# One normalisation for the four mLSTM heads, its factors spread through DRAM, and copied sums of a third projection

## The chip, the cores and the metric

The kernel runs on one core of a Trainium2 chip. Five engines work beside each other, each with its own queue of instructions in a fixed order: TensorE (PE in the profile, with PEld for its weight loads), VectorE (DVE), ScalarE (ACT), GpSimd (POOL) and SyncE (SP). PE multiplies matrices and writes its sums to PSUM, which has eight banks of 128 partitions x 512 float32 numbers. DVE and ACT read PSUM and SBUF, the on-chip memory. SP and POOL here mostly issue transfers between DRAM and SBUF. The metric is device time in microseconds (us); less is better.

## The reference

One layer of a decoder with two token mixers side by side, for 512 tokens of 1024 features in float32:

```python
u = rms_norm(h, norm_mix_g)
z = u @ w_in                      # q, k, v of both mixers and their gates
ya = moba_attention(...)          # 8 heads x 64
hb = mlstm_chunkwise(...)         # 4 heads x 128: num / max(|den|, exp(-m))
hb = hb * rsqrt(mean(hb * hb, axis=-1) + 1e-6)
yb = sigmoid(ob) * (hb * mlstm_norm_g)
merged = sigmoid(ga) * (ya @ w_proj_a) + sigmoid(gb) * (yb @ w_proj_b)
h = h + merged @ w_out
h = h + (silu(g) * up) @ w_down   # g, up = rms_norm(h) @ w_gate_up
return rms_norm(h, norm_final_g)
```

The change is at the second mixer's norm (hb) and at the two products with w_proj. Because the norm divides by the root of the mean square of num / den, the division by den needn't be done by itself: the factor of a token and head is one over the root of (sum of num squared + eps x 128 x max(den squared, floor)), up to powers of two. The floor, exp(-2 m), is a row of 512 numbers for each head.

## The kernel before, in words

All products are taken in three parts, with each float32 operand split into a high and a low half (`split_hl`: ACT copies the high half, DVE subtracts it). The activations lie with features on the partitions and the 512 tokens along the row.

The program is a list of 66 weight units (`UNITS`): q, k, v, ob, qkb, then eight of ga, fourteen half units gs, eight projections p and eight of wo, and behind these the feed-forward network. `fill(1)` issues the next unit on PE: 24 matmuls of 512 columns in most, 12 in a gs unit. The weights' splits run some units ahead on ACT and DVE. Between the units stands the work of the mixers: generators in a list (`add`, `advance`, `drain`), called at written places. From the first stage on, a scheduler orders each engine's instructions by their place in the program and by its own estimate of when their inputs are there; `add_manual_dep(..., behind)` forces an order on one engine, `issue_after` likewise. What it settled is fixed: on the chip every engine goes through its queue in that order.

PSUM is handed out in three pools: `mmb` (3 banks) for units, `sb` (3 banks) for small products, `accb` (2 banks). The gs units hold two of the `sb` banks (Z) from the first S1 product to S4, so one is left in that time.

The mLSTM (lines 1751 to 1853). `ml_load(h)` (1756) fetches a head's rows from the DRAM tensor scr, broadcast to 128 partitions: 1280 numbers of decay weights in three parts, and the floor's 512. `ml_a` and `ml_c` make the weights and the products num (in `accb`) and den (in `sb`; a product with ones, so all 128 partitions hold the same row). Then for each head:

- `ml_d1` (1823): ACT squares num and den and copies num to nsb; DVE takes the maximum of den squared and the floor; the square of num is split.
- `ml_d2` (1832): two matmuls with ones sum the square over the partitions (L1834, L1835); DVE adds eps x 128 x den squared (L1837); ACT takes Ln and Exp for a first inverse root; three DVE instructions of a Newton step (L351 to L353) and one product with nsb (L1843) follow.
- `ml_e` (1846): the sigmoid of ob, the product with the norm's weight and ob (L1852), and the split into yb.

Heads 0 and 1 go through `ml_d2` inside the loop over the mixers' steps, heads 2 and 3 after it (lines 1915 to 1918), with two gs units issued ahead of them; then one unit, `ml_e` of head 0, one unit, `ml_e` of head 1, and so on.

The gs units make gate B by a scheme of seven products (W11, S1, S2, W12, S3, S4, W22, two units each). The results are read from PSUM by ACT or DVE, turned by DVE, written to DRAM by POOL (gd, L663) and read back (gb, L669), in two groups of four.

The projections (`run_p`, 699) take two banks of `mmb` each, pa = ya @ w and pb = yb @ w. `merge` (686) multiplies them by the gates (L689 reads pa, L692 reads pb), adds and splits; `gate` (676) makes the next one's sigmoids. For the first two, ACT first copies pa and pb to SBUF, and both merges come behind the second one's copies; later ones are merged out of PSUM.

Of the kernel before, what the change touches and what calls it, by code (L numbers as in the profile page):

```python
# [8 lines left out]
F32 = mybir.dt.float32  # L9
F32R = mybir.dt.float32r  # L10
BF16 = mybir.dt.bfloat16
AF = mybir.ActivationFunctionType
ALU = mybir.AluOpType
AX = mybir.AxisListType.X

P = 128
S = 512
# [3 lines left out]
BH = 4  # L21
DFF = 2816
FT = DFF // P
EPS = 1e-6
# [15 lines left out]

RS = [slice(0, 512), slice(512, 896), slice(896, 1280), slice(1280, 1792)]
RW = 1792

KR = [(0, slice(0, 512)), (1, slice(0, 384)), (2, slice(0, 256)), (2, slice(256, 384))]

# [8 lines left out]
PORD = (4, 5, 6, 7, 0, 1, 2, 3)  # L54
# [44 lines left out]
def hybrid_layer_kernel(ctx: ExitStack, tc, xT, wall, wgb, wgc, wgu, wds, wdl, g3v, vecs, wgates, consts, rope, out):  # L99
    nc = tc.nc  # L100
    V, A, T = nc.vector, nc.scalar, nc.tensor
# [7 lines left out]
    dram = ctx.enter_context(tc.tile_pool(name="dr", bufs=1, space=bass.MemoryType.DRAM))  # L109
# [7 lines left out]
    def slot(dt=F32, name="a"):  # L117
        return act.tile([P, S], dt, name=nm(name), tag="A")

    def slot4(dt=F32, name="f"):  # L120
        return act.tile([P, 4, S], dt, name=nm(name), tag="A4", bufs=NA4)
# [25 lines left out]
    raw_ins = lambda i: getattr(i, "ins", i)  # L147
# [12 lines left out]
    def act_(out_, in_, func, **kw):  # L160
        if func not in SETS:
            return A.activation(out_, in_, func, **kw)  # L162
        table(SETS[func])
        if ph["manual"]:
            return A.activation(out_, in_, func, **kw)
        with tc.issue_after(ph["load"]):
            i = A.activation(out_, in_, func, **kw)
        ph["ins"].append(raw_ins(i))
        return i

    def split_hl(src, name="h", dst=None):

        h, l = dst or (slot(F32R, name + "h"), slot(F32R, name + "l"))
        last["a"] = act_(h, src, AF.Copy)
        last["v"] = V.tensor_tensor(l, src, f(h), op=ALU.subtract)  # L175
        return h, l
# [171 lines left out]
    def newton(r, v, new, scale=1.0):  # L348

        t = new()  # L350
        V.tensor_tensor(t, r, r, op=ALU.mult)  # L351
        V.scalar_tensor_tensor(t, v, -0.5 * scale, t, op0=ALU.mult, op1=ALU.mult)
        V.scalar_tensor_tensor(t, t, 1.5, r, op0=ALU.add, op1=ALU.mult)  # L353
        return t
# [30 lines left out]
    def drain(g=None):  # L385
        while bulk and (g is None or g in bulk):
            advance()

    def add(g):
        bulk.append(g)  # L390
        return g


    def fill(n=1, mid=None):

        for _ in range(n):
            u = pos[0]
            if u >= len(UNITS):
                if mid:
                    mid()  # L400
                return
            kind, i = UNITS[u]
            while wstate["split"] <= min(u + LOOK + (kind == "gs"), NGEN - 1):
                split_unit()
            pos[0] += 1
            v = u if u < G0 else max(u + G0, 2 * u - 2 * len(GW)) // 2
            make_sums(5 * (min(v, G0) - 19 + max(v - G0 - 10, 0)) // 4)
            g = run[kind](i, *whl.pop(u))
            next(g, None)
            if mid:  # L410
                mid()
            for _ in g:
                pass
# [141 lines left out]
    def silu_batch(idx):  # L555
        for i in idx:
            a = conv[i]
            act_(a, a, AF.Silu)
        table(SETS[AF.Exp])
        for i in idx:  # L560
            if i < 4:
                st["qk", i] = slot4(F32R, "qk")
            t, o = st["qk", i % 4], 2 * (i // 4)
            qkm[i] = split_hl(conv.pop(i), dst=(t[:, o, :], t[:, o + 1, :]))
            yield
# [21 lines left out]
    def load_x():  # L587
        for n, c in (("A", slice(0, 4)), ("B", slice(4, 8))):
            gs[n] = slot4(name="c" + n)
            nc.gpsimd.dma_start(gs[n], xT[c].rearrange("k p s -> p k s"))  # L590
        yield

    def combine():

        for k in range(4):
            x, v = gs["A"][:, k], gs["B"][:, k]
            ng = ng1[:, k : k + 1]
            with tc.issue_after(raw_ins(last["a"])), tc.issue_after(raw_ins(last["v"])):
                act_(v, v, AF.Copy, scale=col(G1 + k + 4))
                V.tensor_tensor(x[:, A_], x[:, A_], x[:, B_], op=ALU.subtract)  # L600
            V.scalar_tensor_tensor(x[:, B_], x[:, B_], ng, v[:, B_], op0=ALU.mult, op1=ALU.add)
            V.scalar_tensor_tensor(v[:, B_], x[:, A_], ng, v[:, B_], op0=ALU.mult, op1=ALU.subtract)
            V.scalar_tensor_tensor(v[:, A_], v[:, B_], -1.0, v[:, A_], op0=ALU.mult, op1=ALU.subtract)
            yield
# [94 lines left out]
    def run_p(m, wh, wl):  # L699
        if m in PORD[4:]:  # L700
            load_xr()
        pa, pb = mmb(), mmb()
        mm3(pa, wh, wl, range(4), [t[0] for t in ya], [t[1] for t in ya], True, True)
        if m == PORD[0]:
            tc.add_manual_dep(raw_ins(st["first"]), raw_ins(st["gs"]).name, behind, reason="order")
        mm3(pb, wh, wl, range(4, 8), [t[0] for t in yb], [t[1] for t in yb], True, True)
        yield
        if m in PORD[:2]:
            q = slot(name="pa"), slot(name="pb")
            for t, z in zip((pa, pb), q):  # L710
                last["g"] = act_(z, t, AF.Copy)
            early.append((m, *q))
            if m == PORD[1]:
                gate(PORD[0])
                for x in early:
                    merge(*x)
        else:
            merge(m, pa, pb)
# [1035 lines left out]
    sc_b = 128.0 ** -0.5  # L1754

    def ml_load(h):
        t = slot4(name="R").rearrange("p b t -> p (b t)")[:, 0:RW]
        nc.gpsimd.dma_start(t, scr[h : h + 1, :].partition_broadcast(P))
        rbc[h] = [t[:, c] for c in RS]

    def ml_w(h):

        ml_load(h)
        yield
        r = rbc[h]
        c = lambda j: cS[:, 4 * j + h : 4 * j + h + 1]
        for j in range(4):
            w = r[KR[j][0]][:, KR[j][1]]
            w = w[:, 0:P]
            V.scalar_tensor_tensor(w, mmask, c(j), w, op0=ALU.subtract, op1=ALU.min)  # L1770
        yield
        for j in range(4):
            w = r[KR[j][0]][:, KR[j][1]]
            act_(w, w, AF.Exp, bias=c(j))
        wready.add(h)
# [29 lines left out]
    def ml_c(h, b, ats):  # L1805
# [12 lines left out]
        if b == 1:  # L1818
            acc[("d", h)] = sb()
            for i in range(2):  # L1820
                T.matmul(acc[("d", h)], onesr, ats[1][i], start=i == 0, stop=i == 1)

    def ml_d1(h):
        num, den = acc.pop(("n", h)), acc.pop(("d", h))
        sqn, d2, nsb = slot(name="sqn"), slot(name="d2"), slot(name="nsb")
        act_(sqn, num, AF.Square)
        act_(d2, den, AF.Square)
        act_(nsb, num, AF.Copy)
        V.tensor_tensor(d2, d2, rbc[h][3], op=ALU.max)
        return split_hl(sqn, "sq"), d2, nsb  # L1830

    def ml_d2(h, sqn, d2, nsb):
        ps = sb()
        T.matmul(ps, onesr, sqn[0], start=True, stop=False)  # L1834
        T.matmul(ps, onesr, sqn[1], start=False, stop=True)  # L1835

        V.scalar_tensor_tensor(d2, d2, EPS * 128.0, ps, op0=ALU.mult, op1=ALU.add)  # L1837

        r = slot(name="ri")
        act_(r, d2, AF.Ln, scale=2.0**-39)  # L1840
        act_(r, r, AF.Exp, scale=-0.5)
        t = newton(r, d2, lambda: slot(name="nt"), 2.0**-39)
        V.scalar_tensor_tensor(t, t, 2.0**-16, nsb, op0=ALU.mult, op1=ALU.mult)  # L1843
        return t

    def ml_e(h, t):

        ob = gz.pop(("ob", h))
        if h >= 2:
            V.tensor_tensor(ob, ob, rb, op=ALU.mult)  # L1850
        act_(ob, ob, AF.Sigmoid)
        V.scalar_tensor_tensor(t, t, col(MG + h), ob, op0=ALU.mult, op1=ALU.mult)  # L1852
        yb[h] = split_hl(t, dst=pair4("yb", h))

# [5 lines left out]

    fill(1)
    qa, qb = [], []
    norms, norms_out = [], {}
    n = 0

    def norm_d2(h, a1):
        norms_out[h] = ml_d2(h, *a1)
        yield

    LA, LC = 3, 1  # L1870
    todo = {
        1: [rope_group("q", 1)], 3: [rope_group("k", 1)], 13: [ml_w(0)], 14: [silu_batch([0, 4, 1, 5])], 16: [ml_w(2)],
        17: [ml_w(1)], 18: [silu_batch([2, 6, 3, 7])], 19: [ml_w(3)], 20: [load_x()], 25: [combine()],
    }
    while n < len(steps) or qa or qb:
        if qa and (len(qa) >= LA or n >= len(steps)):
# [36 lines left out]
    for i in range(4):  # L1913
        ya[i] = split_hl(ya[i], dst=pair4("ya", i))
    fill(2)
    while norms:
        add(norm_d2(*norms.pop(0)[:2]))
    drain()
    for h in range(4):
        if UNITS[pos[0]][0] != "p":  # L1920
            fill(1)
        ml_e(h, norms_out[h])
    while pos[0] < len(UNITS) and UNITS[pos[0]][0] != "p":
        fill(1)
    ffn()
# [100 lines left out]
```

## Time and profile before

| | |
|---|---|
| median of 3 runs | 724.52 us (724.13 to 725.64) |
| the profiled execution | 721.74 us |
| its span, first to last instruction | 720.0 us |
| busy PE / DVE / ACT / POOL | 702.3 / 617.6 / 460.5 / 84.4 us |
| DMA | 170.52 MB, 237 GB/s on average |
| PE busy from 250 to 300 us, and granted clock | 45.49 of 50 us, 0.93 |
| PE busy from 300 to 350 us, and granted clock | 47.79 of 50 us, 1.00 |

Times in the profile count from the span's start. A row in order of time gives start, duration, engine, line, operation, output and inputs, and in brackets how long the engine was idle before it and what released it. Names leave out buffer numbers: `s`, `mm` and `acc` are banks of the three PSUM pools, `d` is a head's den squared, `nt` the Newton tile, `R` the rows that a head loads. PE's rows overlap, since matmuls are pipelined: their distance in time is from start to start.

### The profile page before, as it was taken

To read this page: it belongs to the slowest core of one execution; us is meant where nothing else is said; L and a number is where in the kernel's file an instruction comes from. 1 tells how busy PE (TensorE), PEld (TensorE's weight loads), DVE (VectorE), ACT (ScalarE), POOL (GpSimd) and SP (SyncE) were. 2 spreads that over 40 slices of the span, in tenths; PEclk is the share of its full clock that TensorE was granted. 3 is DMA by queue.
4 is the path that set the end of the run, shared out by engine and by line. 5 is a ranking of instruction groups with operands and counts; after the bars stand their busy time and mean duration, and the time that the engine had idled before them with its cause. 6 is when DMAs were issued, how large, how long until landed. Compare 5 with 4: busy or idle time off the path is not lost.

```text
span 720.0 us, 9618 instructions
## 1 busy us (share of the span) xinstructions
PE 702.3 (98%) x3248; PEld 582.7 (81%) x3248; DVE 617.6 (86%) x1024; ACT 460.5 (64%) x788; POOL 84.4 (12%) x119
## 2 busy tenths in 40 slices
PE   9999999999999989989999999999999999999995
PEld 6888888887888767878888888878888888888884
DVE  6788977898978699958599898898899799797996
ACT  6634888769766598546354756666765666675664
POOL 0013010000011000122020110013003004003000
PEclk9999999999999998999999999999999999999999
DMA  8769595479989783598999548999979649969703
GB/s 322 289 194 237 185 246 170 165 222 319 233 239 341 209 229 117 201 371 262 320 329 271 168 154 226 364 314 266 357 212 275 230 142 216 315 157 272 221 1 117
DMA packets 50849, 170.52 MB, mean 237 GB/s; under 512 B 6348, under 2 KB 6740, under 8 KB 45296
## 3 DMA queue, kind: packets, MB, share of 16 engines
q1 hardware_dynamic: 38320, 124.67, 49.2%
q0 software_dynamic: 12192, 44.69, 28.0%
q8 instruction: 25, 0.41, 0.2%
q10 hardware_dynamic: 288, 0.56, 0.2%
q14 instruction: 24, 0.20, 0.1%
HBM read 145.73 MB, written 64.00 MB: 291 GB/s over the span
## 4 chain that ended last, share of the span: by engine, by line
PE 71%; DVE 17%; ACT 5%; issue 4%; DMA 2%; DVEq 0%; ACTq 0%
PE mm L223 6%; PE mm L227 6%; PE mm L226 5%; PE mm L1009 5%; PE mm L1008 5%; PE mm L1007 5%; PE s L1009 3%; PE s L1008 3%; PE s L1007 3%; PE mm L1252 2%; PE mm L1255 2%; PE mm L1253 2%; DVE wl L175 2%; PE mm L330 2%; DMA cB<-in_xT_dram 2%
## 5 line engine op out<-in xcount | busy, mean ns | idle before, releaser
L162 ACT ACTIVATE w<-raw 128x1024 fp32r<-128x1024 f32 (+2 forms) x107 | 108.1, 1023 | 46.1 <-PE mm L1008 18.9
L982 DVE TENSOR_TENSOR w<-raw,w 128x1024 fp32r<-128x1024 f32 x70 | 84.3, 1219 | 21.7 <-ACT w L162 19.9
L175 DVE TENSOR_TENSOR wl<-raw,wh 128x1024 fp32r<-128x1024 f32 x62 | 75.0, 1216 | 13.3 <-ACT wh L162 12.5
L162 ACT ACTIVATE wh<-raw 128x1024 fp32r<-128x1024 f32 x62 | 65.2, 1055 | 31.8 <-PE mm L226 20.5
L1007 PE MATMUL mm<-w,bq 128*128 128x512 f32 x160 | 62.2, 389 | 0.0
L1009 PE MATMUL mm<-w,bq 128*128 128x512 f32 x160 | 62.2, 389 | 0.0
L1008 PE MATMUL mm<-w,bq 128*128 128x512 f32 x160 | 62.2, 389 | 0.0
L223 PE MATMUL mm<-u,wh 128*128 128x512 f32 x96 | 37.9, 395 | 0.4 <-ACT ga L162 0.4
L227 PE MATMUL mm<-u,wh 128*128 128x512 f32 x96 | 37.5, 391 | 0.0
L226 PE MATMUL mm<-u,wl 128*128 128x512 f32 x96 | 37.5, 390 | 0.0
L227 PE MATMUL mm<-ul,wh 128*128 128x512 f32 x96 | 37.4, 389 | 0.0
L223 PE MATMUL mm<-uh,wh 128*128 128x512 f32 x96 | 37.4, 389 | 0.0
L226 PE MATMUL mm<-uh,wl 128*128 128x512 f32 x96 | 37.3, 389 | 0.0
L1008 PEld LDWEIGHTS mm<-w,bq 128*128 128x128 f32 x160 | 30.0, 188 | 6.3
L1007 PEld LDWEIGHTS mm<-w,bq 128*128 128x128 f32 x160 | 30.1, 188 | 6.2
L1009 PEld LDWEIGHTS mm<-w,bq 128*128 128x128 f32 x160 | 30.0, 188 | 6.2
L1252 PE MATMUL mm<-w,ac 128*128 128x512 f32 x80 | 31.3, 391 | 0.5 <-ACT w L162 0.5
L1163 DVE TENSOR_TENSOR w<-raw,w 128x1024 fp32r<-128x1024 f32 x25 | 30.3, 1216 | 1.3 <-ACT w L162 1.2
L1253 PE MATMUL mm<-w,ac 128*128 128x512 f32 x80 | 31.2, 390 | 0.0
L1007 PE MATMUL s<-w,bq 128*128 128x512 f32 x80 | 31.1, 389 | 0.0
L1008 PE MATMUL s<-w,bq 128*128 128x512 f32 x80 | 31.1, 389 | 0.0
L1009 PE MATMUL s<-w,bq 128*128 128x512 f32 x80 | 31.1, 389 | 0.0
(492 smaller groups left out, 2030.3 us busy)
## 6 DMA issues: line engine op xcount, KB each, us to landing
raw<-in_wall_dram SPq DMA_DIRECT2D x48, 512.0 KB, 5.8
raw<-ws SPq DMA_DIRECT2D x38, 512.0 KB, 6.4
raw<-in_wgc_dram SPq DMA_DIRECT2D x30, 512.0 KB, 7.1
ws<-in_wgc_dram SPq DMA_DIRECT2D x10, 1024.0 KB, 9.8
ws<-in_wgc_dram POOLq DMA_DIRECT2D x10, 1024.0 KB, 11.2
raw<-in_wds_dram SPq DMA_DIRECT2D x15, 512.0 KB, 8.3
ws<-in_wds_dram SPq DMA_DIRECT2D x10, 512.0 KB, 8.3
ws<-in_wds_dram POOLq DMA_DIRECT2D x10, 512.0 KB, 8.5
```

The lines of the kernel that those rows point to most:

```text
L162: return A.activation(out_, in_, func, **kw)
L175: last["v"] = V.tensor_tensor(l, src, f(h), op=ALU.subtract)
L223: st["mm"] = T.matmul(ps, wh[:, c], rh[j], start=start and j == 0, stop=False)
L226: T.matmul(ps, wl[:, c], rh[j], start=False, stop=False)
L227: T.matmul(ps, wh[:, c], rl[j], start=False, stop=stop and j == n - 1)
L982: V.tensor_tensor(l, t, f(h), op=ALU.subtract)
L1007: st["mm"] = T.matmul(ps[t], bh, wh[:, d], start=first and k == 0, stop=False, skip_group_check=not first)
L1008: T.matmul(ps[t], bh, wl[:, d], start=False, stop=False, skip_group_check=not first)
L1009: T.matmul(ps[t], bl, wh[:, d], start=False, stop=k == 3, skip_group_check=not first)
L1163: V.tensor_tensor(w[k][1], g[k], f(w[k][0]), op=ALU.subtract)
L1252: T.matmul(ps, bh, wh[:, d], start=first and k == 0, stop=False, skip_group_check=not first)
L1253: T.matmul(ps, bl, wh[:, d], start=False, stop=False, skip_group_check=not first)
```

## The change

1. `ml_load` leaves the floor out (1280 numbers of a row instead of 1792). A new generator `floors`, behind `load_x` at step 20, loads the four floors into one tile, 32 partitions for each head, by four transfers on POOL's queue.
2. `ml_d1` squares den for its head's 32 partitions of a tile for all four (den4). `ml_d2` keeps only the two matmuls and an ACT copy of the sum's 32 partitions into a tile for all four (ssq4). For heads 2 and 3 the matmuls are ordered behind the last gs matmul issued so far.
3. `ml_norm` makes the maximum, the sum, Ln, Exp and the Newton step once, on the tiles for four heads. It writes one partition of each head to DRAM (8 KB) and reads that back to all 128 partitions for all four heads (1 MB), both on POOL's queue.
4. `ml_e` multiplies nsb by its head's factor (that was the end of `ml_d2`), and goes on as before.
5. The order: two gs units, head 2's sum, one unit, head 3's sum, one unit, `ml_norm`, one unit; then a unit and an `ml_e` for each head. So `ml_e` of head 0 stands behind the seventh gs unit instead of the fourth.
6. The first three projections' sums are copied by ACT instead of the first two, and the first gates and merges come behind the third one's copies.

```diff
-        if m in PORD[:2]:
+        if m in PORD[:3]:
...
-            if m == PORD[1]:
+            if m == PORD[2]:
...
-        t = slot4(name="R").rearrange("p b t -> p (b t)")[:, 0:RW]
-        nc.gpsimd.dma_start(t, scr[h : h + 1, :].partition_broadcast(P))
+        t = slot4(name="R").rearrange("p b t -> p (b t)")[:, 0:RL]
+        nc.gpsimd.dma_start(t, scr[h : h + 1, 0:RL].partition_broadcast(P))
...
+    def floors():
+        row4["m"] = slot(name="fl4")
+        for h in range(BH):
+            nc.gpsimd.dma_start(row4["m"][32 * h : 32 * h + 32, :], scr[h : h + 1, RS[3]].partition_broadcast(32))
+        yield
...
     def ml_d1(h):
...
-        act_(d2, den, AF.Square)
+        act_(row4["d"][r], den[r], AF.Square)
         act_(nsb, num, AF.Copy)
-        V.tensor_tensor(d2, d2, rbc[h][3], op=ALU.max)
...
     def ml_d2(h, sqn):
...
+        if h >= 2:
+            tc.add_manual_dep(raw_ins(i), raw_ins(st["gs"]).name, behind, reason="order")
         T.matmul(ps, onesr, sqn[1], start=False, stop=True)
-        V.scalar_tensor_tensor(d2, d2, EPS * 128.0, ps, op0=ALU.mult, op1=ALU.add)
-        r = slot(name="ri")
-        act_(r, d2, AF.Ln, scale=2.0**-39)
-        act_(r, r, AF.Exp, scale=-0.5)
-        t = newton(r, d2, lambda: slot(name="nt"), 2.0**-39)
-        V.scalar_tensor_tensor(t, t, 2.0**-16, nsb, op0=ALU.mult, op1=ALU.mult)
+        act_(row4["s"][r], ps[r], AF.Copy)
+    def ml_norm():
+        den4, ssq4 = row4["d"], row4["s"]
+        V.tensor_tensor(den4, den4, row4["m"], op=ALU.max)
+        V.scalar_tensor_tensor(den4, den4, EPS * 128.0, ssq4, op0=ALU.mult, op1=ALU.add)
+        act_(ssq4, den4, AF.Ln, scale=2.0**-39)
+        act_(ssq4, ssq4, AF.Exp, scale=-0.5)
+        t = newton(ssq4, den4, lambda: row4["m"], 2.0**-39)
+        d = dram.tile([BH, S], F32, name="nd4")
+        nc.gpsimd.dma_start(d, t.rearrange("(h r) t -> h r t", r=32)[:, 0, :])
+        row4["b"] = slot4(name="nb4")
+        nc.gpsimd.dma_start(row4["b"], d.rearrange("h t -> (h t)").partition_broadcast(P).rearrange("p (h t) -> p h t", h=BH))
     def ml_e(h):
...
+        t = row4["n", h]
+        V.scalar_tensor_tensor(t, row4["b"][:, h], 2.0**-16, t, op0=ALU.mult, op1=ALU.mult)
         V.scalar_tensor_tensor(t, t, col(MG + h), ob, op0=ALU.mult, op1=ALU.mult)
...
-        1: [rope_group("q", 1)], ..., 20: [load_x()], 25: [combine()],
+        1: [rope_group("q", 1)], ..., 20: [load_x(), floors()], 25: [combine()],
...
     fill(2)
+    drain()
     while norms:
+        fill(1)
         add(norm_d2(*norms.pop(0)[:2]))
-    drain()
+        drain()
+    fill(1)
+    ml_norm()
+    fill(1)
     for h in range(4):
         if UNITS[pos[0]][0] != "p":
             fill(1)
-        ml_e(h, norms_out[h])
+        ml_e(h)
```

More of the change, by code (lines that the diff above doesn't have):

```diff
@@ L42 @@
 RW = 1792
+RL = 1280
 KR = [(0, slice(0, 512)), (1, slice(0, 384)), (2, slice(0, 256)), (2, slice(256, 384))]
@@ L1756, in ml_load @@
     def ml_load(h):
-        t = slot4(name="R").rearrange("p b t -> p (b t)")[:, 0:RW]
-        nc.gpsimd.dma_start(t, scr[h : h + 1, :].partition_broadcast(P))
-        rbc[h] = [t[:, c] for c in RS]
+        t = slot4(name="R").rearrange("p b t -> p (b t)")[:, 0:RL]
+        nc.gpsimd.dma_start(t, scr[h : h + 1, 0:RL].partition_broadcast(P))
+        rbc[h] = [t[:, c] for c in RS[:3]]
     def ml_w(h):
@@ L1821, in ml_c @@
                 T.matmul(acc[("d", h)], onesr, ats[1][i], start=i == 0, stop=i == 1)
+    row4 = {}
+    def floors():
[3 more added lines that the diff above has]
+        yield
     def ml_d1(h):
         num, den = acc.pop(("n", h)), acc.pop(("d", h))
-        sqn, d2, nsb = slot(name="sqn"), slot(name="d2"), slot(name="nsb")
+        sqn, nsb = slot(name="sqn"), slot(name="nsb")
+        r = slice(32 * h, 32 * h + 32)
@@ L1826, in ml_d1, with ml_d2 @@
         act_(sqn, num, AF.Square)
-        act_(d2, den, AF.Square)
+        if h == 0:
+            row4["d"] = slot(name="den4")
+        act_(row4["d"][r], den[r], AF.Square)
         act_(nsb, num, AF.Copy)
-        V.tensor_tensor(d2, d2, rbc[h][3], op=ALU.max)
-        return split_hl(sqn, "sq"), d2, nsb
-    def ml_d2(h, sqn, d2, nsb):
+        row4["n", h] = nsb
+        return split_hl(sqn, "sq")
+    def ml_d2(h, sqn):
         ps = sb()
-        T.matmul(ps, onesr, sqn[0], start=True, stop=False)
+        i = T.matmul(ps, onesr, sqn[0], start=True, stop=False)
+        if h >= 2:
+            tc.add_manual_dep(raw_ins(i), raw_ins(st["gs"]).name, behind, reason="order")
@@ L1835, in ml_d2 @@
         T.matmul(ps, onesr, sqn[1], start=False, stop=True)
-        V.scalar_tensor_tensor(d2, d2, EPS * 128.0, ps, op0=ALU.mult, op1=ALU.add)
-        r = slot(name="ri")
-        act_(r, d2, AF.Ln, scale=2.0**-39)
-        act_(r, r, AF.Exp, scale=-0.5)
-        t = newton(r, d2, lambda: slot(name="nt"), 2.0**-39)
-        V.scalar_tensor_tensor(t, t, 2.0**-16, nsb, op0=ALU.mult, op1=ALU.mult)
-        return t
-    def ml_e(h, t):
+        r = slice(32 * h, 32 * h + 32)
+        if h == 0:
+            row4["s"] = slot(name="ssq4")
@@ L1848, in ml_e @@
+    def ml_e(h):
         ob = gz.pop(("ob", h))
@@ L1862, in hybrid_layer_kernel @@
     qa, qb = [], []
-    norms, norms_out = [], {}
+    norms = []
     n = 0
     def norm_d2(h, a1):
-        norms_out[h] = ml_d2(h, *a1)
+        ml_d2(h, a1)
         yield
@@ L1872, in hybrid_layer_kernel @@
         1: [rope_group("q", 1)], 3: [rope_group("k", 1)], 13: [ml_w(0)], 14: [silu_batch([0, 4, 1, 5])], 16: [ml_w(2)],
-        17: [ml_w(1)], 18: [silu_batch([2, 6, 3, 7])], 19: [ml_w(3)], 20: [load_x()], 25: [combine()],
+        17: [ml_w(1)], 18: [silu_batch([2, 6, 3, 7])], 19: [ml_w(3)], 20: [load_x(), floors()], 25: [combine()],
     }
```

## The prediction, made before the result was known

> **What bounds the kernel now.** I read the page's busy times first, then the list of what TensorE (PE) waited for, then stretches of 5 us around its longest wait.
>
> ```profile
> PE 702.3 (98%) x3248; PEld 582.7 (81%) x3248; DVE 617.6 (86%) x1024; ACT 460.5 (64%) x788; POOL 84.4 (12%) x119
> ```
>
> PE is busy for 98% of the 720.0 us span, so only idle PE time, or PE time at a lower clock, can be won. Two waits hold most of what is idle inside the program (engine, line, waited for: us in total, times, longest):
>
> ```profile
> PE s L1834 <- DVE d L1837: 4.5, 1, 4.5
> ...
> PE mm L223 <- DVE ga L689: 2.2, 1, 2.2
> ```
>
> Both touch edited lines. The stretches give busy time by engine, then granted clock, DMA share, GB/s:
>
> ```profile
> 260.00:265.00 5.00, 5.00 (x24) 4.12 (x23) 5.00 (x9) 4.77 (x11) 0.00 (x0) 1.00 0.97 279
> 265.00:270.00 5.00, 1.63 (x8) 1.00 (x6) 5.00 (x9) 4.89 (x10) 0.00 (x0) 0.93 0.35 120
> 270.00:275.00 5.00, 3.86 (x9) 3.11 (x10) 4.76 (x10) 2.27 (x5) 0.00 (x0) 0.50 0.57 179
> ...
> 320.00:325.00 5.00, 2.79 (x13) 2.01 (x12) 4.97 (x9) 4.20 (x9) 0.04 (x1) 1.00 0.98 329
> ```
>
> From 260 to 270 VectorE (DVE) is busy without a break, and ScalarE (ACT) nearly so. PE stops, and after the stop its granted clock is 0.50. PE in order of time (start, duration, engine, line):
>
> ```profile
> 264.87 0.40 PE L1834 MATMUL s<-sqh,onesr 128*128 128x512 f32 x1
> ...
> 266.24 0.39 PE L634 MATMUL s<-wl,u 128*128 128x512 f32 x1
> 271.14 0.77 PE L1834 MATMUL s<-sqh,onesr 128*128 128x512 f32 x1 [4.51 <-DVE d L1837]
> ...
> 276.29 0.40 PE L633 MATMUL mm<-wh,u 128*128 128x512 f32 x1
> ...
> 302.85 0.39 PE L223 MATMUL mm<-ya,wh 128*128 128x512 f32 x1
> ...
> 305.57 0.39 PE L223 MATMUL mm<-yb,wh 128*128 128x512 f32 x1
> ...
> 324.26 0.50 PE L223 MATMUL mm<-yb,wh 128*128 128x512 f32 x1 [2.21 <-DVE ga L689]
> ```
>
> The sum of squares of the third head (264.87) and of the fourth (271.14) share the one PSUM bank that the gate's products leave. The fourth waits until DVE has read the third, and DVE comes to that late:
>
> ```profile
> 270.32 0.68 DVE L1837 SCALAR_TENSOR_TENSOR d<-d,s 128x512 f32<-128x512 f32 x1
> ```
>
> The wait is 4.5 us. The clock costs more: from 302.85 to 305.57 are 12 matmuls, 0.227 us each; from 271.14 to 276.29 are also 12, which take 5.15 instead of 2.72 us, so 2.4 us are lost. First wait: **6.9 us**. The second, 2.2 us at 324.26, is the second product of projection 3 (counted from 0) waiting for a bank that projection 2's merge has yet to read; the clock stayed at 1.00 there.
>
> **The Trainium skill on this.** "TensorE: Matmul & The Clock Gate", HAM oscillation, says that idle gaps above about 3.4 us put PE back to half clock for about a window. The trace agrees: 4.51 us brought 0.50, 2.21 us did not. It speaks against any change that puts a long wait elsewhere; the sum is the same without it, since the 2.4 us are measured.
>
> **The change, part by part.** Durations (min/median/max ns):
>
> ```profile
> L162 ACT ACTIVATE nsb<-acc x4: 598/602/605, 227.2 to 264.5; 128x512 f32<-128x512 f32 x4
> ...
> L167 ACT ACTIVATE ri<-d x4: 614/624/633, 252.3 to 274.0; 128x512 f32<-128x512 f32 x4
> ...
> L1843 DVE SCALAR_TENSOR_TENSOR nt<-nt,nsb x4: 678/682/683, 257.3 to 280.8; 128x512 f32<-128x512 f32 x4
> L1852 DVE SCALAR_TENSOR_TENSOR nt<-nt,vec,ob x4: 739/742/743, 280.1 to 289.0; 128x512 f32<-128x512 f32 x4
> L162 ACT ACTIVATE yb<-nt x4: 624/630/642, 281.3 to 289.8; 128x512 fp32r<-128x512 f32 x4
> L175 DVE TENSOR_TENSOR yb<-nt,yb x4: 675/682/691, 281.9 to 291.5; 128x512 fp32r<-128x512 f32 x4
> ```
>
> *DVE.* Per head six 512-wide instructions go (maximum, sum, three of Newton, product): 24 x 0.68 = 16.3 us. Back come five for all heads and four products, 9 x 0.68 = 6.1 us, so 10.2 us less. Two heads' chains and three maxima, 13 instructions or 8.8 us, lie ahead of 270.32, where DVE is full.
>
> *ACT.* Eight Ln and Exp become two, and four copies of the sums come in: 6 x 0.62 - 4 x 0.60 = 1.3 us less. The squares of the denominators and the copies run on 32 partitions. No row shows that width with 512 columns; a quarter of the work bounds them at 0.15 us below, the full-width row at 0.60 above. I take 0.60, the same number of columns.
>
> *PE.* The eight small matmuls stay. Heads 2 and 3 are ordered behind whole gate units: the seven matmuls left of the interrupted unit come first, 266.47 + 7 x 0.227 = 268.1. Head 3's bank must by then be read by the ACT copy of head 2, whose matmuls end at about 265.5. ACT is full there, without an idle mark from its first row to its second:
>
> ```profile
> 264.98 0.65 ACT L162 ACTIVATE sqh<-sqn 128x512 fp32r<-128x512 f32 x1
> ...
> 269.45 0.44 ACT L162 ACTIVATE u<-cA 128x256 fp32r<-128x256 f32 x1
> ```
>
> The copy is issued somewhere from 265.5 to 269.9, so it ends from 266.1 to 270.5. Up to 268.1 it costs nothing. I take nothing: it stands in the program ahead of the next units' weight splits, two of which are in that queue. The later end is a rival below. Then PE stands **6.9 us** earlier, at 296.0 for the first projection and 298.7 for its first use of yb.
>
> *The new wait.* yb now needs the whole chain. Head 3's sum ends at 268.8. The copy takes 0.6 to 2.1 us, with up to 1.5 us of queue. Maximum sum, Ln, Exp and Newton take 4 x 0.68 + 2 x 0.62 = 4.0 us back to back; the same chain of the last head took 7.8 us, from the first row here to the end of the second:
>
> ```profile
> 272.37 0.69 DVE L1837 SCALAR_TENSOR_TENSOR d<-d,s 128x512 f32<-128x512 f32 x1 [0.24 <-PE s L1835]
> ...
> 279.49 0.68 DVE L353 SCALAR_TENSOR_TENSOR nt<-nt,ri 128x512 f32<-128x512 f32 x1
> ```
>
> So the factors are ready from 273.4 to 278.7; I take 276.5, nearer the measured chain. Then 8 KB go to DRAM and 1 MB comes back broadcast, both on POOL's queue. The nearest rows (issue rows of a small write and of the read that waits for it; then KB each, us to landing):
>
> ```profile
> 418.32 0.52 POOL L1127 DMA_DIRECT2D row<-vec  x1 [7.70 <-DVE vec L353]
> 421.03 0.74 POOL L1128 DMA_DIRECT2D rg<-row  x1 [2.19 <-DMA row<-vec]
> ...
> ws<-in_wgb_dram SPq DMA_DIRECT2D x2, 1024.0 KB, 5.2
> R<-scr POOLq DMA_DIRECT2D x4, 896.0 KB, 11.5
> cA<-in_xT_dram POOLq DMA_DIRECT2D x1, 1024.0 KB, 14.6
> scr<-rr POOLq DMA_DIRECT2D x2, 8.0 KB, 7.3
> ```
>
> Write: 2.7 to 7.3 us. I take 4, since DMA is less loaded here (share 0.35 and 0.57) than where the 7.3 us arose. Broadcast: 5.2 to 14.6 us; R is the same kind of transfer, and with lighter load I take 10. It lands at 290.5 (bounds 281.3 and 300.6). Each head then needs 0.68 + 0.74 + 0.68 = 2.1 us of DVE and 0.63 us of ACT; four heads in a pipeline, 4 x 2.1 + 0.6 = 9.0 us, end at 299.5. DVE shares this time with the gate's sums. Before, it read product S4 (DVE row) 3.6 us behind its end, which is where the last product begins (PE row):
>
> ```profile
> 297.41 0.39 PE L633 MATMUL mm<-wh,u 128*128 128x512 f32 x1
> ...
> 300.97 1.40 DVE L658 SCALAR_TENSOR_TENSOR gS<-s,rt,gS 128x512 f32<-128x512 f32 x2
> ```
>
> I add these 3.6: 303.1. PE uses head 3's half from 298.7 + 9 x 0.227 = 300.7. New wait: **2.4 us** (nothing to 12.5). What stands behind the waiting product on DVE is the gate's sums and the weight splits; the splits run several units ahead, the gate's sums do not, so they are late next.
>
> *Gates.* The third projection's copies (2 x 0.60 us of ACT, beside PE) free the bank behind the 2.2 us. The gate's rows (POOL, ACT, DVE, each in order of time):
>
> ```profile
> 253.78 0.81 POOL L848 DMA_DIRECT2D ws<-in_wgc_dram  x1 [5.64 <-PE mm L226]
> 303.87 2.65 POOL L663 DMA_DIRECT2D gd<-gt  x4 [49.29 <-DVE gt L659]
> ...
> 319.11 0.63 ACT L167 ACTIVATE gb<-gb 128x512 f32<-128x512 f32 x1 [3.35 <-DMA gb<-gd]
> ...
> 330.12 0.63 ACT L167 ACTIVATE gb<-gb 128x512 f32<-128x512 f32 x1 [2.33 <-DMA gb<-gd]
> ...
> 325.32 0.68 DVE L689 TENSOR_TENSOR ga<-mm,ga 128x512 f32<-128x512 f32 x1
> ...
> 333.48 0.68 DVE L689 TENSOR_TENSOR ga<-mm,ga 128x512 f32<-128x512 f32 x1
> ```
>
> S4 now ends on PE at 297.41 - 6.9 = 290.5; its way to DRAM began 6.5 us behind that (303.87), and one head of the new products ahead of it on DVE adds 2.1, so 299.1. The first gates came 15.2 us after this (319.11), so 314.3; projection 3's read ended 6.9 us after them. But the merges now begin behind projection 2's copies: 296.0 + 2.4 + 3 x 5.44 + 0.6 = 315.3 (a projection is 24 matmuls, 5.44 us), so projection 3 is read at 322.2. Projection 4's second product needs that bank at 296.0 + 2.4 + 4 x 5.44 + 2.7 = 322.9: hidden, **2.2 us won**. The second group of gates came 26.3 us after the start (330.12), and projection 4's read ended 4.0 us later: 329.4. Projection 5's second product wants that bank at 328.3: **1.1 us lost** (nothing to 3).
>
> *Other DMAs.* The four loads of R shrink by 256 KB each, four of 64 KB come in, and the broadcast is 1 MB: 0.25 MB more of 170 MB. POOL issues nothing between 253.78 and 303.87, so no transfer queues behind the two new ones. Cost nothing; without that cover, the wait for the write (up to 7.3 us) would delay POOL's next issue.
>
> *Sum.* -6.9 + 2.4 - 2.2 + 1.1 = -5.6 us. The profiled execution took 721.74 us, so 716.1; it lies 2.8 below the median 724.52, on whose scale I forecast **718.9 us**. Later stages issue their loads relative to PE, so they should move as a block.
>
> **Rivals.** *A, the broadcast is hidden and DVE keeps pace.* At the 5.2 us row it lands at about 285.7, yb is ready by 298.3 and the gates are not pushed back: only -6.9 - 2.2 = -9.1 us, **715.4**. For it: DMA share 0.35 to 0.57. Against: all four R loads were slower. "DMA: Bandwidth & Descriptors" of the Trainium skill, Anatomy of one DMA, gives 2.0 us plus bytes over 436 GB/s, 2.0 and 4.4 us here by my estimate, which is this case; the trace's rows are longer.
>
> *B, the change does not free the bank.* If ACT's queue holds the copy to 270.5, PE still waits 2.4 us behind 268.1, too short for the clock to fall by the second wait's row. All else shifts alike: **721.3**. For it: ACT 4.89 of 5 us busy; against: 1.3 us of its work goes.
>
> *C, slower: the trip through DRAM outlasts the gate units.* At the upper bounds the broadcast lands at 300.6 and head 3 is ready at 313.2: 12.5 us of wait plus 2.4 us of low clock, minus 9.1 (after so long a wait all gates come in time), gives 5.8 us more, **730.3**. The gain is gone when wait and clock reach 9.1 us, at a wait of 6.7 us, so when the broadcast lands after 294.8. Against: that takes 4.3 us more than I allow. For it: DVE waits in order, and the gate's reads behind it would stop PE even earlier.
>
> **How the numbers follow.** Forecast 0.56 (its own range 716.5 to 721), A 0.18, B 0.13, C 0.13. Range 714.6 to 724.5: from A's time with some spread to C's turning point. A measurement here can tell about 0.2% (1.4 us) from no change. Faster: forecast, A, and most of B and early C, 0.79; same 0.09, where a wait eats the rest; slower 0.12.
>
> **What would show it.** Right: no wait of L1834's matmul, clock 1.00 from 265 to 280, the first projection some 7 us earlier, and a short wait of L223 or L226 on yb. Wrong: a PE wait for ACT at the sums (B), none at yb (A), over 4 us there with a low clock (C), or PE waiting behind DVE's gate reads while DVE waits for the broadcast.

## The result, and the profile after

On one chip, in turns, the changed kernel took 716.66 us (median of 4 runs, 715.20 to 719.07) and the kernel before 724.33 (4 runs, 723.00 to 725.64): ratio 0.990, 95% interval 0.986 to 0.994. The forecast was 718.9 us. The profiled execution took 719.07 us, with a span of 717.3; before it was 721.74 and 720.0. It is the longest of its four, and two more profiles of the same kernel stand with the experiments.

The page's busy times, and what PE waited for (engine, line, waited for: us in total, times, longest):

```profile
PE 700.4 (98%) x3248; PEld 580.7 (81%) x3248; DVE 610.0 (85%) x1009; ACT 461.6 (64%) x788; POOL 87.7 (12%) x125
...
PE mm L224 <- ACT mgh L163: 1.5, 1, 1.5
PE mm L634 <- DVE gS L659: 1.4, 1, 1.4
PE mm L635 <- DVE wl L176: 1.3, 1, 1.3
PE mm L224 <- DVE gb L693: 1.1, 1, 1.1
PE mm L224 <- DVE ga L690: 1.0, 1, 1.0
```

No row names the sums of squares any more. Five short waits have come in place of the two long ones: two in the gate units (L634, L635) and three from the projections on (L224). These three stand at the second product of projection 4 (323.43 us), at the first of projection 6 (332.97) and in the first unit of wo (348.62, the row with mgh), with projections counted from 0; at projection 3 PE waits no more. DVE has the 15 instructions less that the change removes and is busy 7.6 us less. In stretches of 5 us (columns: busy PE, PEld, DVE, ACT, POOL, granted clock, DMA share, GB/s), the places of the old waits and of the new ones:

```profile
235.00:240.00 5.00, 5.00 (x24) 4.14 (x23) 4.93 (x14) 2.90 (x5) 0.00 (x0) 1.00 0.68 204
...
245.00:250.00 5.00, 5.00 (x27) 4.22 (x26) 3.09 (x5) 4.15 (x8) 0.82 (x1) 1.00 0.70 170
...
265.00:270.00 5.00, 5.00 (x23) 4.09 (x22) 3.76 (x7) 4.81 (x10) 0.00 (x0) 1.00 0.57 191
270.00:275.00 5.00, 5.00 (x24) 4.13 (x23) 4.02 (x9) 4.97 (x9) 0.00 (x0) 1.00 0.60 194
...
290.00:295.00 5.00, 3.44 (x14) 2.55 (x14) 5.00 (x8) 2.53 (x3) 0.00 (x0) 1.00 0.19 59
```

PE is full from 265 to 275, at a clock of 1.00 where it had 0.50. But there is something that the prediction did not have: DVE is busy from 235 to 240, and not full from 245 on. The kernel before has it the other way round. Its stretches, and the first ACT row behind the idle time:

```profile
235.00:240.00 5.00, 5.00 (x23) 4.12 (x22) 0.00 (x0) 0.71 (x2) 0.00 (x0) 1.00 1.01 291
...
245.00:250.00 5.00, 5.00 (x27) 4.22 (x26) 5.00 (x10) 2.60 (x6) 0.83 (x1) 1.00 0.19 29
```

```profile
239.29 0.72 ACT L162 ACTIVATE cB<-cB,vec 128x512 f32<-128x512 f32 x1 [5.58 <-DMA cB<-in_xT_dram]
```

Before, ACT stood 5.58 us waiting for the second half of the input (cB, `load_x`), and DVE stood behind ACT. The work of `combine` on that half then fell together with the norm, and from 245 to 270 DVE was full. POOL's queue says why. Its issues before:

```profile
212.40 0.81 POOL L590 DMA_DIRECT2D cA<-in_xT_dram  x1 [1.48 <-PE s L1791]
...
227.64 0.81 POOL L590 DMA_DIRECT2D cB<-in_xT_dram  x1 [9.40 <-PE s L1791]
```

and after, with the two new transfers behind them:

```profile
203.17 0.80 POOL L591 DMA_DIRECT2D cA<-in_xT_dram  x1 [0.89 <-PE acc L1742]
205.66 0.78 POOL L591 DMA_DIRECT2D cB<-in_xT_dram  x1 [1.69 <-DVE R L1771]
...
275.37 0.60 POOL L1865 DMA_DIRECT2D nd<-fl  x1 [22.11 <-DVE fl L354]
277.36 0.58 POOL L1867 DMA_DIRECT2D nb<-nd  x1 [1.38 <-DMA nd<-fl]
```

cB starts 22.0 us earlier. The heads' rows R, the halves cA and cB and some of the q and k tiles share eight tiles of one size (`slot4`). The floor was the part of R that was read last, by the maximum in `ml_d1`. Without it a head's R is done with once its decay weights are multiplied in and split, and cA and cB no longer wait for a product of q and k (the releaser L1791 of before). Which tile went to which load is read from the code and the releasers; that the floor in R decides it is tested below.

The trip through DRAM (KB, us from issue to landing), and DVE at its end and at the gate sum that PE then waited for:

```profile
nb<-nd POOLq DMA_DIRECT2D x1, 1024.0 KB, 6.8
nd<-fl POOLq DMA_DIRECT2D x1, 8.0 KB, 1.7
```

```profile
284.17 1.29 DVE L1876 SCALAR_TENSOR_TENSOR nsb<-nb,nsb 128x512 f32<-128x512 f32 x2 [0.99 <-DMA nb<-nd]
...
289.70 0.74 DVE L659 SCALAR_TENSOR_TENSOR gS<-mm,nrt,gS 128x512 f32<-128x512 f32 x1
...
297.66 0.68 DVE L176 TENSOR_TENSOR yb<-nsb,yb 128x512 fp32r<-128x512 f32 x1
```

The factors were on all partitions at 284.2, and the last half of yb was ready at 298.3. PE in order of time:

```profile
290.59 0.47 PE L634 MATMUL mm<-wh,u 128*128 128x512 f32 x1 [1.38 <-DVE gS L659]
295.34 0.50 PE L635 MATMUL mm<-wl,u 128*128 128x512 f32 x1 [1.31 <-DVE wl L176]
297.74 0.39 PE L224 MATMUL mm<-ya,wh 128*128 128x512 f32 x1
...
300.46 0.39 PE L224 MATMUL mm<-yb,wh 128*128 128x512 f32 x1
```

PE began its products with yb at 300.46 without a wait. It had waited before that, for a gate sum and a weight split that DVE did late among the new products.

### The profile page after: what moved, and what is told of

Its sections match the earlier page's. It is cut to its first block, busy times and chain, and to the rows that moved or that the text cites. A ratio compares the mean times of both kernels' runs of the same rounds, so it can differ in the third digit from the quotient of the medians.

```text
span 717.3 us, 9632 instructions
## 1 busy us (share of the span) xinstructions
PE 700.4 (98%) x3248; PEld 580.7 (81%) x3248; DVE 610.0 (85%) x1009; ACT 461.6 (64%) x788; POOL 87.7 (12%) x125
## 4 chain that ended last, share of the span: by engine, by line
PE 69%; DVE 16%; ACT 5%; DMA 4%; issue 4%; POOL 1%; POOLq 0%; DVEq 0%; ACTq 0%
PE mm L228 5%; PE mm L224 5%; PE mm L227 5%; PE mm L1008 5%; PE mm L1009 5%; PE mm L1010 5%; PE s L1009 3%; PE s L1008 3%; PE s L1010 3%; DMA gd<-gt 2%; PE mm L1253 2%; PE mm L1254 2%; PE mm L1256 2%; DVE wl L176 2%; PE mm L331 2%
## 5 line engine op out<-in xcount | busy, mean ns | idle before, releaser
L224 PE MATMUL mm<-u,wh 128*128 128x512 f32 x96 | 37.8, 394 | 0.0
L224 PE MATMUL mm<-uh,wh 128*128 128x512 f32 x96 | 37.4, 389 | 0.0
```

What stands on the lines that cost most here:

```text
L224: st["mm"] = T.matmul(ps, wh[:, c], rh[j], start=start and j == 0, stop=False)
```

## The experiments

All times are medians, and each ratio is against runs of the kernel before on the same chip in the same sitting. There were three sittings. In the first, with the changed kernel again, the floors alone, the floors in R and the change with two copies, the kernel before took 722.17 us; in the second, with the three copies alone, floors and copies, the longer trip and the factor last, 722.11; in the third, with the changed kernel once more and the writes first, 722.09 (23, 23 and 24 runs, from 719.3 to 726.0).

**The changed kernel again.** Nothing edited, in two sittings.

> The changed kernel once more, unchanged. Its four runs lie between 715.2 and 719.07 us, wider than those of before. If the spread comes from transfers that land a little earlier or later, the sums' wait stays away in this profile too, the clock is 1.00 from 265 to 280 us, and the small waits of the profile shown (1.38 and 1.31 us in the gate units, 1.05 and 1.08 in the projections, 1.54 at the first wo unit) change by up to a us each, with a sum of 3 to 6.3 us. The time is 716.7 us, give or take 1.5.

> The changed kernel once more, beside the three below on one chip. By the five runs so far 715 to 717 us, about 0.9925 of the kernel before; waits of PE of 0.8 to 1.5 us at the gate sums (L659), at a weight split (L176) and at the merges (L690).

Measured: 715.69 us, ratio 0.9926 (0.9897 to 0.9955), and 716.13 us, 0.9913 (0.9881 to 0.9946). What PE waited for in the first of these executions, which took 715.41 us:

```profile
PE mm L634 <- DVE gS L659: 1.5, 1, 1.5
PE mm L635 <- DVE wl L176: 1.3, 1, 1.3
...
PE mm L224 <- DVE ga L690: 0.8, 1, 0.8
```

The two waits in the gate units are steady. Those at projection 6 and at mgh, 2.6 us in the first profile, come and go between executions.

**The floors alone.** The kernel before, with the floors taken out of R and loaded into four tiles of 128 partitions at step 20. The norm stays one for each head, nothing of it goes through DRAM, and two projections are copied.

```diff
-        t = slot4(name="R")...[:, 0:RW]
+        t = slot4(name="R")...[:, 0:1280]
...
+    def floors():
+        for h in range(BH):
+            fl4[h] = slot(name="fl")
+            nc.gpsimd.dma_start(fl4[h], scr[h : h + 1, RS[3]].partition_broadcast(P))
...
-        V.tensor_tensor(d2, d2, rbc[h][3], op=ALU.max)
+        V.tensor_tensor(d2, d2, fl4[h], op=ALU.max)
...
-        20: [load_x()],
+        20: [load_x(), floors()],
```

> The kernel before, with one part of the change alone: the floors are loaded into tiles of their own (four of 128 partitions) at step 20, so the tiles R are free as soon as the decay weights are used. The norm stays per head, with all its DVE instructions. By the prediction's theory (DVE has too many norm instructions ahead of the read of the bank) the wait at the fourth head's sum stays at 4 to 5 us with the clock at 0.50, and the time at 724 us. By the rival (R's early release lets the load of x be issued some 20 us earlier, at about 206 instead of 227.6 us, so that DVE does that load's work while it has room, and its full stretch from 240 to 270 us is gone) the wait is under 1 us, the clock 1.00, and the time about 6.9 us less, 717.5 us, with the 2.2 us wait in the projections still there.

Measured: 715.41 us, 0.9907 (0.9875 to 0.9938), as fast as the whole change. Its waits and its issue of cB:

```profile
PE mm L223 <- DVE ga L689: 1.6, 1, 1.6
...
PE s L1843 <- DVE d L1846: 0.2, 1, 0.2
```

```profile
207.11 0.78 POOL L590 DMA_DIRECT2D cB<-in_xT_dram  x1 [2.22 <-DVE R L1770]
```

The stretch of the old wait, and the fourth head's sum:

```profile
265.00:270.00 5.00, 4.80 (x22) 3.65 (x21) 5.00 (x9) 4.31 (x9) 0.00 (x0) 1.00 0.42 144
```

```profile
267.36 0.47 PE L1843 MATMUL s<-sqh,onesr 128*128 128x512 f32 x1 [0.20 <-DVE d L1846]
```

With cB 20.5 us earlier the wait at the sums (L1843 here) falls from 4.51 to 0.2 us, though each head keeps its whole chain on DVE. Nothing of the norm has to change for it. The expectation that DVE's full stretch would go was wrong: from 260 to 270 DVE is as full as before. But the work of `combine` is over by 247.5 instead of 252.1, and DVE reads the third head's sum at 266.54 instead of 270.32. The run moves the load by moving the floors, and DVE's order of work was settled anew with it; the time of the load was not varied by itself.

**The floors left in R.** The changed kernel with R at 1792 numbers again and without `floors`; the maximum is taken for each head, on its 32 partitions.

```diff
-RL = 1280
+RL = 1792
...
+        V.tensor_tensor(row4["d"][r], row4["d"][r], rbc[h][3][r], op=ALU.max)
...
-        V.tensor_tensor(den4, den4, row4["m"], op=ALU.max)
...
-        20: [load_x(), floors()],
+        20: [load_x()],
```

> The changed kernel with that part undone: the floors come with R again, so each R is held until its head's denominator is squared, and the maximum is taken per head on 32 partitions (three DVE instructions more). The norm is still taken once. By the prediction's theory no wait appears at the sums, and the time is that of the changed kernel, 716.7 us. By the rival the second half of x is loaded at about 227 us again, DVE is full from 240 to 270, and PE waits 1 to 4.5 us somewhere between 260 and 275: 719 to 723 us.

Measured: 720.09 us, 0.9977 (0.9956 to 0.9997). Issue of cB, stretches (columns as above) and two PE rows of its profiled execution:

```profile
228.07 0.81 POOL L591 DMA_DIRECT2D cB<-in_xT_dram  x1 [9.40 <-PE s L1792]
```

```profile
265.00:270.00 5.00, 5.00 (x24) 4.05 (x23) 3.73 (x7) 4.93 (x10) 0.00 (x0) 1.00 0.67 252
...
294.00:297.00 3.00, 3.00 (x9) 2.41 (x8) 3.00 (x6) 2.02 (x3) 0.00 (x0) 0.53 0.02 5
...
351.00:354.00 3.00, 2.54 (x8) 1.99 (x8) 1.42 (x2) 0.41 (x1) 0.00 (x0) 0.70 0.94 212
```

```profile
292.95 0.47 PE L634 MATMUL mm<-wh,u 128*128 128x512 f32 x1 [1.99 <-DVE gS L659]
...
351.46 0.50 PE L224 MATMUL mm<-mgh,wh 128*128 128x512 f32 x1 [1.55 <-ACT mgh L163]
```

cB is late again, and still PE doesn't wait at the sums: the norm taken once, with ACT reading the bank, is also enough by itself. But only 2.1 us are gained (722.17 - 720.09), for the work returns in the gate units: 1.99 us at the gate sum, then lost clock. The execution shown took 723.44 us, the longest of ten, so these waits may be larger than the median run's. Against the changed kernel in the same sitting the floors in R cost 720.09 - 715.69 = 4.4 us. That difference holds three more maxima on DVE too, which this run can't take apart from the late load.

**Three copies, alone and taken away.** The kernel before with a third projection copied (first), the changed kernel with two (second), and the floors alone with a third copy (third).

```diff
-        if m in PORD[:2]:
+        if m in PORD[:3]:
...
-            if m == PORD[1]:
+            if m == PORD[2]:
```

> The kernel before with the third projection's copies alone. The 4.5 us wait at the sums stays, and the clock falls there. By the prediction the 2.2 us wait at projection 3 goes and a later one of some 1 us comes: 1 us less than before. By the rival that the earlier run with two copies suggests (the first gates arrive far behind the third projection, and the copies are worth the whole 5 to 6 us that it lost) the gain is at most the 2.2 us there is to win here.

> The changed kernel with two projections' sums copied as before, instead of three. By the prediction the third copy is worth 2.2 us less the later wait that it uncovers, 1.1: the wait before projection 3's second product comes back at 1 to 3 us, the later ones shrink, and the time is 717 to 719 us. By the rival (the gate's way through DRAM sets the projections' end, and a copy only moves the wait) the sum of PE's waits from 297 to 350 us stays at 3.7 us within 0.7, and the time is 716.7 us.

> The kernel before with the floors in tiles of their own and the third projection's copies; the norm per head, without the trip through DRAM. If the norm taken once is worth nothing by itself, this is at or under the run with the floors alone (715.4 us): its 1.6 us wait at projection 3 goes, 714 us. If the norm taken once matters for the projections, the time is 715.4 or more.

Measured: 719.26 us, 0.9965 (0.9945 to 0.9985), for the kernel before with three; 721.34, 0.9985 (0.9966 to 1.0004), for the changed kernel with two; 714.62, 0.9906 (0.9875 to 0.9937), for floors and three copies. The sums' wait in the first and the stretch behind it, and the longest wait of the second:

```profile
270.03 0.77 PE L1834 MATMUL s<-sqh,onesr 128*128 128x512 f32 x1 [4.12 <-DVE d L1837]
```

```profile
270.00:275.00 5.00, 4.97 (x12) 3.94 (x13) 4.18 (x7) 3.29 (x6) 0.00 (x0) 0.50 0.57 204
```

```profile
PE mm L224 <- DVE ga L690: 6.1, 1, 6.1
```

The copy leaves the first wait and its low clock alone and is worth 2.9 us by itself (722.11 - 719.26). In the changed kernel it is worth 721.34 - 715.69 = 5.7 us: without it the wait at projection 3 is not 2.2 but 6.1 us. Both branches of the expectation missed that. The rows say where it comes from: the first projection begins 5.39 us earlier than in the kernel before (297.46 against 302.85), but ACT's first sigmoid of gate B only 1.45 us (317.66 against 319.11), and 2.21 + 5.39 - 1.45 = 6.15. With the floors alone, which has two copies as well, POOL issues the gate's first write at 298.63 instead of 301.35, that sigmoid stands at 313.04, and the wait is 1.64 us. So in the changed kernel the gate's way through DRAM is late against the projections. That DVE's products behind the broadcast hold it up is likely, but was not tried by itself. On the floors alone it adds nothing that the intervals show. So floors and copies, without a line of the new norm, reach the ratio of the whole change.

**A longer trip.** The changed kernel with the 8 KB of factors copied twice more within DRAM before they are spread.

```diff
+        d2 = dram.tile([BH, S], F32, name="nd5")
+        nc.gpsimd.dma_start(d2, d)
+        d = dram.tile([BH, S], F32, name="nd6")
+        nc.gpsimd.dma_start(d, d2)
```

> The changed kernel with the trip through DRAM lengthened by two more copies of the 8 KB from DRAM to DRAM, each behind the one before, some 2.3 us each; the broadcast lands about 4.6 us later, at 289 us instead of 284. By the prediction's sum the broadcast has room until PE uses the fourth head's yb (ready at 298.3 in the profile, used at 302.5), so the time stays within 1 us of 715.7. By the rival (DVE waits for the broadcast in order, and the gate's read of product S3 stands behind it) PE's wait at the last gate product grows from 1.4 to 5 or 6 us, the clock falls, and the time is 720 to 723 us.

Measured: 720.15 us, 0.9968 (0.9945 to 0.9990). DVE where the factors land, the PE row that waits, and two ACT rows:

```profile
292.30 1.29 DVE L1880 SCALAR_TENSOR_TENSOR nsb<-nb,nsb 128x512 f32<-128x512 f32 x2 [3.73 <-DMA nb<-nd]
```

```profile
303.96 0.79 PE L224 MATMUL mm<-yb,wh 128*128 128x512 f32 x1 [6.65 <-ACT g L163]
```

```profile
299.21 1.29 ACT L163 ACTIVATE yb<-nsb 128x512 fp32r<-128x512 f32 x2 [3.63 <-DVE nsb L1881]
...
303.25 1.24 ACT L163 ACTIVATE g<-mm,nrt 128x512 f32<-128x512 f32 x2
```

The factors land 8.1 us later (292.30 against 284.17), where 4.6 were expected: the broadcast is issued 5.5 us later (282.84 against 277.36) and itself takes 9.4 instead of 6.8 us. That costs 3.0 us by the ratios (0.42% of 722), 4.5 by the medians of two sittings. PE waits 6.65 us, put down to ACT's reading of a gate product's bank (g), and in ACT's queue (last fence) that reading stands behind the splits into yb, which wait for DVE's products with the factors.

**The factor last.** The changed kernel with the two products of `ml_e` exchanged, so that the product with the weight and ob doesn't need the broadcast.

```diff
-        V.scalar_tensor_tensor(t, row4["b"][:, h], 2.0**-16, t, ...)
         V.scalar_tensor_tensor(t, t, col(MG + h), ob, ...)
+        V.scalar_tensor_tensor(t, row4["b"][:, h], 2.0**-16, t, ...)
```

> The changed kernel with the two products of yb in the other order: first nsb with the norm's weight and the sigmoid, which are there early, then the factor from DRAM. DVE has 0.7 to 0.8 us less for each head behind the landing, and does it in the idle time ahead. If the small waits in the gate units come from DVE's load behind the broadcast, both shrink, 1.4 to 0 and 1.3 to under 1 us, and the time is 1.5 to 2.5 us under the changed kernel's 715.7. If they come from the order on DVE alone, they stay and the time is 715.7.

Measured: 713.87 us (713.32 to 717.73), 0.9900 (0.9865 to 0.9935). Its waits:

```profile
PE mm L224 <- DVE ga L690: 1.0, 1, 1.0
...
PE mm L635 <- DVE wl L176: 0.7, 1, 0.7
```

The wait at gate sum S4's bank (gS) is gone and the one at the weight split is half, as DVE does a part of the products before the factors land. So both came from the products that DVE had to do behind the landing, or from the order in which it did them, which changed with the edit. Whether the kernel is faster than the changed one, the intervals don't say.

**Both groups of gate B written first.** POOL issues all eight writes of gate B ahead of the first read: on the changed kernel, on that with the factor last, and on floors with three copies.

```diff
-            for m in range(4):
-                z = gz["gb", 4 * n + m] = slot(name="gb")
-                nc.gpsimd.dma_start(z, d[m * P : (m + 1) * P, :])
+            gs["d", n] = d
+        if w == "W22":
+            for n in (1, 0):
+                for m in range(4):
+                    z = gz["gb", 4 * n + m] = slot(name="gb")
+                    i = nc.gpsimd.dma_start(z, gs["d", n][m * P : (m + 1) * P, :])
```

> The changed kernel with both groups of gate B written to DRAM before the first group is read back; POOL's write of the second group then no longer stands behind the reads, which wait for the first write. If the waits at projections 4 and 5 (1.05 and 1.08 us, on the gates' way) come from that queue, both shrink and the kernel takes about 1 us less than the changed one. If they come from DVE's order of work alone, no change.

> The changed kernel with the factor multiplied last in the products before yb, and both writes of gate B ahead of the reads. If the wait of 1.38 us at gate sum S4 comes from DVE standing behind the broadcast, it goes here too, and with the gates' waits the sum is 1.4 + 1 = 2.4 us less than the changed kernel. If the gain of the factor alone (713.87 against 715.69) was chance of the runs, no more than 1 us.

> The kernel before with the floors out of R, three copies, and both writes of gate B ahead of the reads; the norm stays one for each head and nothing of it goes through DRAM. If the changed kernel's gain is that of the floors and the copies alone, it is as fast as the changed kernel or up to 1.5 us faster (714 to 716). If the norm taken once is worth something of its own, the kernel with factor last and the same writes is over 1 us faster than this.

Measured: 719.62 us, 0.9961 (0.9941 to 0.9981); 718.59, 0.9949 (0.9929 to 0.9969); 715.81, 0.9901 (0.9872 to 0.9931). The first two miss: slower than the changed kernel (716.13 us in this sitting), by 3.5 and 2.5 us. ACT's first gate row and the reads' time to landing in the changed kernel:

```profile
316.09 0.63 ACT L168 ACTIVATE gb<-gb 128x512 f32<-128x512 f32 x1 [0.16 <-DMA gb<-gd]
```

```profile
gb<-gd POOLq DMA_DIRECT2D x8, 256.0 KB, 5.1
```

and with the writes first:

```profile
319.86 0.63 ACT L168 ACTIVATE gb<-gb 128x512 f32<-128x512 f32 x1 [3.08 <-DMA gb<-gd]
```

```profile
gb<-gd POOLq DMA_DIRECT2D x8, 256.0 KB, 8.8
```

```profile
PE mm L224 <- DVE ga L695: 3.8, 1, 3.8
```

The first reads are issued no earlier (312.09 against 312.30), since they wait for their own writes, and the reads land in 8.8 instead of 5.1 us (medians of eight), probably because the second group's writes now go just ahead of them. So the first gate comes 3.8 us later, and projection 4's second product waits 3.8 us (last row). For the third kernel there is no measurable difference to 0.9906 without the writes. No kernel here is shown to beat the changed one; the floors alone equal it with a fraction of the edit.

## Why the prediction was right, and where not

The terms, beside what the two profiled executions of the changed kernel show (us, from the rows above; the first and third lines are what the kernel before lost there, since nothing is lost there now):

| term | forecast | 719.07 us run | 715.41 us run |
|---|---|---|---|
| wait and clock at the sums | -6.9 | -6.9 | -6.9 |
| new wait for DVE behind the broadcast | +2.4 | 1.38 + 1.31 = +2.7 | 1.5 + 1.3 = +2.8 |
| projection 3 (third copy) | -2.2 | -2.2 | -2.2 |
| projection 4, taken as hidden | 0 | +1.0 | +0.8 |
| projection 5 in the forecast, 6 in the run | +1.1 | +1.1 | 0 |
| mgh, not foreseen | 0 | +1.5 | 0 |
| sum | -5.6 | -2.8 | -5.5 |
| execution against 721.74 | | -2.7 | -6.3 |

So the rows give the gain to about a microsecond. The sum of -5.6 is a little short of the differences of medians, from 5.96 (722.09 - 716.13) to 7.7 us (724.33 - 716.66). The time of 716.66 lies at the lower end of its own range of 716.5 to 721, and nearer to rival A's 715.4 than to 718.9. Step by step it is a mixed account, and in part luck: the sum left out a cause as large as the whole forecast, and still came out because that cause removes the same wait that the sum had already given to the norm.

Of the signs that were named, the sums' wait is gone and the clock is 1.00 from 265 to 280. The first projection begins 5.1 us earlier (297.74 against 302.85) and not 7, since the new waits stand ahead of it. The wait on yb did not come.

**The first wait: right in size, incomplete in cause.** The prediction gave its end to 13 fewer norm instructions on DVE and to ACT reading the bank. The floors left in R show that this is enough. The floors alone show that it isn't needed. In the changed kernel both work, but with the floors left in R 2.1 us of gain remain, and the floors alone give 6.8. Its count of DVE's relief was too high as well: 15 instructions less made DVE 7.6 us less busy, not 10.2. Back to back, rows of 0.68 us start 0.60 us apart (252.00 and 252.60 in the kernel before), so 15 of them are 9.0 us at most.

**"Cost nothing" for the other DMAs: the step that failed.** It counted the bytes of the floors' loads and the queue that they pass, but not that a shorter R is done with earlier, and who waits for its tile. That is a gain of about the size of the whole forecast: 722.17 - 715.41 = 6.8 us alone, and 4.4 us inside the change. The sign was in the trace: ACT's idle 5.58 us on cB, and DVE's empty stretch at 235 ahead of its full one, stand ahead of the stretches from 260 on that the prediction shows.

**The new wait: right in size, wrong in place.** The factors left at 275.37 (forecast 276.5); the write landed in 1.7 us (taken: 4) and the broadcast in 6.8 (taken: 10), so they were there at 284.2, not 290.5. At yb itself nothing waited, 298.3 against the 303.1 of the forecast. But the sentence that the gate's sums "are late next" is what happened, at 290.59, and a weight split followed. I had named it without giving it a price, and called the splits several units ahead; one was not. That the two errors nearly cancel (2.4 against 2.7) is luck. For the write and the broadcast, "DMA: Bandwidth & Descriptors" of the Trainium skill, Anatomy of one DMA, gave 2.0 and 4.4 us by the estimate in the prediction: the trace's 1.7 for the write is near it, and its 6.8 for the broadcast lies between that estimate and my 10.

**The copies: right at projection 3, short at the next.** The wait at projection 3 is gone, as forecast. But projection 4's second product, which the sum took as hidden with 0.7 us to spare (322.9 against 322.2), waits 1.05 and 0.77 us: its turn came at 322.2, and projection 3's sum was read at 323.4. The gate's way to DRAM began at 301.65, where 299.1 was forecast. The later loss of 1.1 us came one product further on than forecast, at projection 6's first, and in one of the two executions. Taken away from the changed kernel, the copy proves to be worth 5.7 us, not 2.2 less 1.1, so the change as it stands depends on it.

**ACT at 32 partitions: right.** A copy of 32 partitions and 512 columns takes about as long here as one of 128, 0.60 in the prediction's row:

```profile
246.76 0.57 ACT L163 ACTIVATE ssq<-s 32x512 f32<-32x512 f32 x1
```

**The rivals.** A (no wait at yb) was right on the trip: it had the landing at 285.7 and yb ready by 298.3, and the run has 284.2 and 298.3. But DVE did not keep pace with the gate's sums. B is out: no row has PE waiting for ACT at the sums. C was tried by the longer trip. At a landing of 292.3 the kernel still gains 722.11 - 720.15 = 2.0 us, and each microsecond of delay took from 3.0 / 8.1 = 0.37 to 4.5 / 8.1 = 0.55; on these lines, an estimate, the gain would be gone from 295.9 to 297.7, somewhat behind C's 294.8. PE then stopped behind the read of a gate's bank, as C said, though it was ACT's read and not DVE's.

## What to carry to other kernels

When a part of a tile is moved out, ask which read was the tile's last and which load takes the tile next: that load may be worth more than the work that was edited. Look for an engine's idle time ahead of its full stretch, not only inside it, since a late load there pushes its work into the full one. And try the smallest side of a change alone: here the floors' part gave as much as the whole, and all the rest without it 2 us of 722.

## What was not expected of the hardware

Short waits also cost clock. In the execution shown of the kernel with the floors left in R, the longest of its ten, a wait of 1.99 us was followed by a granted clock of 0.53 from 294 to 297, and one of 1.55 us by 0.70 from 351 to 354, while the 2.21 us of the kernel before left it at 1.00, and 1.38 and 1.31 us within 5 us of each other did too. "TensorE: Matmul & The Clock Gate" of the Trainium skill, HAM oscillation, puts the limit at gaps of about 3.4 us; 4.12 and 4.51 us, each followed by 0.50, agree with it; 1.99 and 1.55 us don't. What else decides was not tried, so a wait under that length can't be taken as free of it, and the spread between runs of one kernel may come from there; that is not shown.
